# One more tile pair by seven block products in the first group of each MLP

## The chip, the cores and the metric

One core of a Trainium2 chip runs the whole program, once. Its engines each work through a list of their own, in order: TensorE (PE) multiplies, VectorE (DVE), ScalarE (ACT) and GpSimd (POOL) work element by element, SyncE (SP) issues the loads. The metric is the device time of one execution in microseconds (us), as a median over runs.

## The reference, cut to what matters

Three blocks follow one another on 528 tokens (16 meta tokens and 512 real ones) of width 1024: differential attention, latent attention, and a mixer with convolution and window attention. Behind each stands the same gated MLP, and the change is in these three MLPs alone:

```python
xn = rms_norm(h, g_norm)
a, b = jnp.split(xn @ w_in, 2, axis=-1)          # w_in: 1024 x (2 * 2816)
a_conv = conv_b + sum(ap[:, j:j + L] * conv_w[j] for j in range(3))   # along the tokens
return h + (jax.nn.silu(a_conv) * b) @ w_out     # w_out: 2816 x 1024
```

The 2816 hidden features are 22 tiles of 128. A tile pair is tile f of `a` together with tile f of `b`: two products of a 1024 x 128 weight tile with all tokens.

## The kernel before, in words

Features lie on the 128 partitions and tokens along the row. The normalised rows are divided by their root mean square only after the product, by a row R. Every operand of a large product is held as a high part and the remainder (`whi`/`wlo`, `Xh`/`Xl`), and a product is three matmuls: high by high, high by low, low by high. ACT casts the high part of a weight (line 176), DVE or POOL subtracts for the low part (lines 184 and 114).

An MLP is `ffn` (line 519). Its 22 tile pairs run in four groups, listed in the table `GROUPS` (line 61); behind each group its part of the second product (`group_h`) is added to h. A number in the table is a **plain** pair (class `Plain`): 2 tiles x 2 token halves x 8 chunks of 128 inputs x 3 matmuls = 96 matmuls of 256 to 264 columns. Pair 0 is a plain pair of its own form, `opening`, which also works out R. A tuple goes through `turns` (line 705): its last member is a plain pair, the others are of class `Seven`. A Seven pair takes the two weight tiles, the two halves of the 1024 inputs and the two token halves as a 2 x 2 by 2 x 2 product of blocks and makes it with seven block products in place of eight. A block product (`block`, line 565) is 4 chunks x 3 = 12 matmuls, so a Seven pair has 84. Its steps are named p1 to p7 in the code; p1 and p5 come first.

The seven products need sums and differences on both sides:

- Of the weights: `plan_ffn` loads four tiles' worth as kinds "a", "s", "t", "d"; `combine` (line 132) lets POOL add and subtract raw halves (`rawS`, `raw_0`, `raw_1`), and `_split` casts them. A Seven pair has 3.5 tiles to split where a plain pair has 2.
- Of the tokens: `differences` (line 540) makes, once for each MLP, four combinations of the blocks of X for k = 0 to 3: ACT scales (line 545), DVE makes `d` (lines 552, 553, 556, 557), ACT casts it into `Th` (562), DVE writes the remainder into `Tl` (563). p5 is the first step that reads `Th` and `Tl`: the first combination for all four k, in order of k. p1 reads X itself.

What sets the order: PE's instructions of `opening` and of each `turns` stand as they are written. The order of ACT, DVE, POOL and SP, and of PE elsewhere, is laid down when the program is built, by a scheduler that works from its own estimates; on the chip each engine then goes strictly through its list and waits on semaphores. Weights pass through 3 raw buffers and 4 split buffers; "s" and "d" have one buffer of their own.

The work of the other lines named below: 608 and 632 multiply the product in PSUM by R (`am`), 581, 585, 588 and 589 are the convolution, SiLU and R of the gate (`ct`), 612 and 642 multiply by the other tile's product, 450 and 451 split the result (`Gh`, `Gl`).

```python
u = [Seven(f, f - k0) for f in fs[:-1]]
v = Plain(fs[-1], fs[-1] - k0)
x, y = u[0], u[-1]
x.p1(), x.p5(), v.a(0), x.p6(), x.p2(), v.a(1), x.p7()
if x is y:
    v.b(0), x.p3(), x.p4(), v.b(1)
    return
x.p3(), y.p1(), x.p4(), y.p5(), y.p6(), y.p2(), v.b(0), y.p7(), y.p3(), v.b(1), y.p4()
```

Of the kernel before, what the change touches and what calls it, by code (L numbers as in the profile page):

```python
# [42 lines left out]
def _layout_params():  # L43
# [15 lines left out]
NPAR = _layout_params()  # L59

GROUPS = (
    (0, 5, (0, 1, 2, (3, 4))),
    (5, 10, ((5, 6, 7), (8, 9))),
    (10, 16, ((10, 11, 12), (13, 14, 15))),
    (16, 22, ((16, 17, 18), (19, 20, 21))),
# [1897 lines left out]
```

## Time and profile before

| | |
|---|---|
| median of 3 runs | 2063.59 us (2060.54 to 2064.36) |
| the profiled execution | 2064.14 us, of which 2062.4 us are the span from the first to the last instruction |
| PE busy | 2036.0 us, 99% of the span |
| DVE, ACT, POOL busy | 68%, 48%, 35% of the span |
| granted TensorE clock | 0.995 of 2.4 GHz on average |

The page gives busy time by engine. The chain of waits, in order of time, says which engine the end was waiting for at each moment. The timeline lists single instructions with start and length; the windows give busy time in a stretch. An engine that is busy 68% of the span on average may still be full in one stretch.

### The profile page before, as it was taken

What the parts mean: (1) busy time and instruction counts of PE and PEld (TensorE: products, weight loads), DVE (VectorE), ACT (ScalarE), POOL (GpSimd) and SP (SyncE); (2) the same over time, 40 slices, a digit from 0 to 9 for tenths busy, and PEclk for the clock granted to TensorE, in tenths of its full rate; (3) what the DMA queues carried; (4) which work ended last, traced back from release to release, by engine and by line L of the source; (5) the groups of instructions that cost most, each with busy time, mean ns of one, the idle gap of its engine ahead of it and who ended that gap; (6) DMA issues with size and microseconds to landing.
All of it is one profiled execution on the core that took longest, in us unless ns stands there. A gap on an engine that the chain in (4) does not pass through costs nothing.

```text
span 2062.4 us, 36284 instructions
## 1 busy us (share of the span) xinstructions
PE 2036.0 (99%) x14314; PEld 1884.8 (91%) x14314; DVE 1400.2 (68%) x2548; ACT 980.5 (48%) x1967; POOL 719.1 (35%) x818
## 2 busy tenths in 40 slices
PE   8999999999999999999999999999999999999998
PEld 8999899999999989899899898888888889999897
DVE  8788768667677576668667687675433358667684
ACT  6666545434355455455435355454332335445353
POOL 5222252435353331132536355321022242436452
PEclk9999999999999999999999999999999999999999
DMA  5121132333323111032332322222223232322322
GB/s 172 53 62 52 42 105 68 106 93 98 99 84 98 53 41 42 32 99 74 100 102 92 110 85 89 87 92 72 67 81 104 97 113 70 105 93 99 116 72 72
DMA packets 56426, 174.91 MB, mean 85 GB/s; under 512 B 6464, under 2 KB 9408, under 8 KB 56256
## 3 DMA queue, kind: packets, MB, share of 16 engines
q1 hardware_dynamic: 55824, 172.34, 26.4%
q8 instruction: 112, 1.84, 0.4%
q14 instruction: 58, 0.48, 0.1%
q10 hardware_dynamic: 432, 0.27, 0.0%
HBM read 170.45 MB, written 2.10 MB: 84 GB/s over the span
## 4 chain that ended last, share of the span: by engine, by line
PE 87%; DVE 8%; ACT 2%; issue 1%; POOL 1%; DMA 0%; ACTq 0%; DVEq 0%; SPq 0%
PE po L343 24%; PE pf L576 18%; PE pf L343 17%; PE pc L343 6%; PE pg L343 4%; PE pyc L343 2%; PE pq L343 2%; PE s L767 2%; DVE wlo L184 2%; PE ph L343 2%; PE pm L343 2%; PE pd L343 1%; PE o L1422 1%; PE pya L343 1%; DVE nm L777 1%
## 5 line engine op out<-in xcount | busy, mean ns | idle before, releaser
L176 ACT CAST whi<-raw 128x512 fp32r<-128x512 f32 (+4 forms) x484 | 384.7, 808 | 532.9 <-PE po L343 154.5
L114 POOL TENSOR_TENSOR wlo<-raw,whi 128x256 fp32r<-128x256 f32 (+1 forms) x316 | 273.9, 894 | 572.7 <-ACT whi L176 537.3
L184 DVE TENSOR_TENSOR wlo<-raw,whi 128x512 fp32r<-128x512 f32 (+2 forms) x590 | 410.7, 731 | 50.6 <-ACT whi L176 47.3
L343 PE MATMUL pf<-Xl,whi 128*128 128x256 f32 (+2 forms) x960 | 271.2, 283 | 0.9 <-DVE Xl L454 0.9
L343 PE MATMUL pf<-Xh,whi 128*128 128x256 f32 (+2 forms) x960 | 271.4, 283 | 0.0
L343 PE MATMUL pf<-Xh,wlo 128*128 128x256 f32 (+2 forms) x960 | 271.4, 283 | 0.0
L343 PE MATMUL po<-Gh,wlo 128*128 128x512 f32 (+2 forms) x710 | 239.4, 338 | 0.0
L343 PE MATMUL po<-Gl,whi 128*128 128x512 f32 (+2 forms) x710 | 238.5, 337 | 0.0
L343 PE MATMUL po<-Gh,whi 128*128 128x512 f32 (+2 forms) x710 | 235.6, 340 | 0.0
L343 PEld LDWEIGHTS pf<-Xl,whi 128*128 128x128 f32 x960 | 181.3, 189 | 1.2 <-DVE Xl L454 1.1
L343 PEld LDWEIGHTS pf<-Xh,whi 128*128 128x128 f32 x960 | 181.6, 189 | 0.0
L343 PEld LDWEIGHTS pf<-Xh,wlo 128*128 128x128 f32 x960 | 181.6, 189 | 0.0
L576 PE MATMUL pf<-Tl,whi 128*128 128x264 f32 (+2 forms) x576 | 162.4, 282 | 0.0
L576 PE MATMUL pf<-Th,whi 128*128 128x264 f32 (+2 forms) x576 | 162.3, 282 | 0.0
L576 PE MATMUL pf<-Th,wlo 128*128 128x264 f32 (+2 forms) x576 | 162.3, 282 | 0.0
L343 PEld LDWEIGHTS po<-Gh,wlo 128*128 128x128 f32 x710 | 133.5, 188 | 16.8
L343 PEld LDWEIGHTS po<-Gl,whi 128*128 128x128 f32 x710 | 133.6, 188 | 15.2
L343 PEld LDWEIGHTS po<-Gh,whi 128*128 128x128 f32 x710 | 132.5, 188 | 14.8
L576 PE MATMUL pf<-Xh,whi 128*128 128x264 f32 (+2 forms) x432 | 121.9, 282 | 0.0
L576 PE MATMUL pf<-Xh,wlo 128*128 128x264 f32 (+2 forms) x432 | 121.9, 282 | 0.0
L576 PE MATMUL pf<-Xl,whi 128*128 128x264 f32 (+2 forms) x432 | 121.9, 282 | 0.0
L585 DVE SCALAR_TENSOR_TENSOR ct<-am,par,ct 128x512 f32<-128x512 f32 (+4 forms) x132 | 114.5, 867 | 5.6 <-ACT ct L581 4.6
(434 smaller groups left out, 5496.3 us busy)
## 6 DMA issues: line engine op xcount, KB each, us to landing
raw<-in_w_in_dram SPq DMA_DIRECT2D x134, 512.0 KB, 3.5
raw<-in_w_up_dram SPq DMA_DIRECT2D x44, 512.0 KB, 3.3
raw<-in_w_qkv_dram SPq DMA_DIRECT2D x24, 512.0 KB, 3.6
raw<-in_w_out_dram SPq DMA_DIRECT2D x32, 384.0 KB, 3.2
raw<-in_w_out_dram SPq DMA_DIRECT2D x32, 320.0 KB, 2.9
raw<-in_w_o_dram SPq DMA_DIRECT2D x16, 512.0 KB, 3.5
raw<-in_w_dn_dram SPq DMA_DIRECT2D x16, 384.0 KB, 3.2
raw<-in_w_dn_dram SPq DMA_DIRECT2D x16, 320.0 KB, 2.9
```

The lines of the kernel that those rows point to most:

```text
L114: self.net.nc.gpsimd.tensor_tensor(d[:, c], a[:, c], b[:, c], op=op)
L176: nc.scalar.copy(h[:, c0 : c0 + z], r)
L184: nc.vector.tensor_tensor(l[:, c], r[:, a:b], h[:, c].bitcast(F32), op=ALU.subtract)
L343: nc.tensor.matmul(ps, w, x, start=first and i == 0, stop=i == len(ops) - 1, skip_group_check=not first)
L576: nc.tensor.matmul(ps[:, :H], a, b, start=first and i == 0, stop=i == len(ops) - 1, skip_group_check=not first)
L585: nc.vector.scalar_tensor_tensor(t[:, z:], am[:, a : a + n - z], w, t[:, z:], op0=ALU.mult, op1=ALU.add)
L767: nc.tensor.matmul(s[:, :w], qa[:, q0 : q0 + P], ka[:, k0:k1], start=z == 0, stop=z == len(ops) - 1 and not masked,)
L777: nc.vector.reduce_max(nm[:, j : j + 1], s[:, :w], axis=AX.X, negate=True)
L1422: nc.tensor.matmul(o[:, i, j, :], st[n, "pt", j][:, b * P : (b + 1) * P], V[:, b, c], start=n % 4 == j == b == 0, stop=False,)
```

## The change: the first group's table

```diff
 GROUPS = (
-    (0, 5, (0, 1, 2, (3, 4))),
+    (0, 5, (0, 1, (2, 3, 4))),
     (5, 10, ((5, 6, 7), (8, 9))),
     (10, 16, ((10, 11, 12), (13, 14, 15))),
     (16, 22, ((16, 17, 18), (19, 20, 21))),
```

Pair 2 of each MLP turns from a plain pair into a Seven pair. It takes its turns with Seven pair 3 and plain pair 4, in the form that (5, 6, 7) has already. Two plain pairs, 0 and 1, are left ahead of the first Seven pair, in place of three.

PE in the first MLP, where plain pair 1 ends (`pf` are the products; whi_4084 is pair 1's second weight). Before:

```order
L343 MATMUL pf_4314<-Xh_3587,wlo_4085 128x264
L343 MATMUL pf_4357<-Xh_3587,whi_4214 128x264
...
L343 MATMUL pf_4449<-Xh_3587,wlo_4280 128x264
L576 MATMUL pf_4485<-Xh_3587,whi_4343 128x264
...
L576 MATMUL pf_4508<-Th_4006,whi_4415 128x264
L576 MATMUL pf_4508<-Tl_4007,whi_4415 128x264
```

PE at the same place now (whi_4216 is pair 2's "a" weight, whi_4288 its "s" weight):

```order
L343 MATMUL pf_4322<-Xh_3587,wlo_4085 128x264
L576 MATMUL pf_4358<-Xh_3587,whi_4216 128x264
...
L576 MATMUL pf_4383<-Th_4006,whi_4288 128x264
L576 MATMUL pf_4383<-Tl_4007,whi_4288 128x264
```

The 96 matmuls of plain pair 2 are gone from between pair 1 and the first p1; p5, the first reader of `Th` and `Tl`, now stands 12 matmuls behind pair 1.

DVE in the first MLP, at the end of the differences (d_4203 and d_4204 are those of k = 3; Tl from d_4203 is the last that p5 needs). Before:

```order
L563 TENSOR_TENSOR Tl_4007<-d_4180,Th_4006 128x2x264
L563 TENSOR_TENSOR Tl_4007<-d_4191,Th_4006 128x2x264
L563 TENSOR_TENSOR Tl_4007<-d_4192,Th_4006 128x2x264
L556 TENSOR_TENSOR d_4203<-d_4204,x_4201 128x264
L184 TENSOR_TENSOR wlo_4501<-raw_1_4286,whi_4500 128x512
L184 TENSOR_TENSOR wlo_4501<-raw_0_4284,whi_4500 128x512
L585 SCALAR_TENSOR_TENSOR ct_4273<-am_4213,par,ct_4273 128x527
L557 SCALAR_TENSOR_TENSOR d_4204<-h,par,d_4203 128x264
L632 TENSOR_TENSOR am_4342<-pf_4357,R_4008 128x264
L632 TENSOR_TENSOR am_4342<-pf_4383,R_4008 128x264
L563 TENSOR_TENSOR Tl_4007<-d_4203,Th_4006 128x2x264
```

DVE now (d_4205 and d_4206 are those of k = 3, d_4193 and d_4194 of k = 2):

```order
L184 TENSOR_TENSOR wlo_4399<-raw_0_4379,whi_4398 128x512 x2
L553 SCALAR_TENSOR_TENSOR d_4206<-h,par,x_4203 128x264
L556 TENSOR_TENSOR d_4193<-d_4194,x_4191 128x264
L556 TENSOR_TENSOR d_4205<-d_4206,x_4203 128x264
L557 SCALAR_TENSOR_TENSOR d_4194<-h,par,d_4193 128x264
L632 TENSOR_TENSOR am_4215<-pf_4230,R_4008 128x264
L632 TENSOR_TENSOR am_4215<-pf_4256,R_4008 128x264
L557 SCALAR_TENSOR_TENSOR d_4206<-h,par,d_4205 128x264
L563 TENSOR_TENSOR Tl_4007<-d_4193,Th_4006 128x2x264
L563 TENSOR_TENSOR Tl_4007<-d_4205,Th_4006 128x2x264
```

From the first `am` (line 608) to the last `Tl` that p5 needs, DVE had 43 instructions and now has 37: gone from this stretch are two of line 184, two of line 632, one of line 585 and one of line 563. In the second MLP it is 44 and 39 (three of line 184 and two of line 632 fewer), in the third 43 and 39 (three of line 184 and two of line 632 fewer, one of line 585 more).

POOL in the first MLP, from the weights of the first Seven pair on (raw_0_4284 and raw_1_4286 are pair 3). Before:

```order
L114 TENSOR_TENSOR rawS_4348<-raw_1_4286 128x256 x2
L114 TENSOR_TENSOR wlo_4616<-raw_1_4286,whi_4615 128x256 x2
L400 TENSOR_TENSOR nr_4057<-nv_4055,mhalf 128x5
L114 TENSOR_TENSOR rawS_4995<-raw_1_4954 128x256 x2
L114 TENSOR_TENSOR raw_1_4286<-raw_0_4284,raw_1_4286 128x256 x2
L114 TENSOR_TENSOR raw_0_4284<-rawS_4348,raw_0_4284 128x256 x2
L114 TENSOR_TENSOR raw_0_4284<-raw_0_4284 128x256 x2
```

POOL now (4091 and 4093 are pair 2, 4379 and 4381 pair 3):

```order
L114 TENSOR_TENSOR rawS_4221<-raw_1_4093 128x256 x2
L114 TENSOR_TENSOR wlo_4500<-raw_1_4093,whi_4499 128x256 x2
L400 TENSOR_TENSOR nr_4057<-nv_4055,mhalf 128x5
L114 TENSOR_TENSOR rawS_4403<-raw_1_4381 128x256 x2
L114 TENSOR_TENSOR raw_1_4093<-raw_0_4091,raw_1_4093 128x256 x2
L114 TENSOR_TENSOR raw_1_4381<-raw_0_4379,raw_1_4381 128x256 x2
L114 TENSOR_TENSOR raw_0_4091<-rawS_4221,raw_0_4091 128x256 x2
L114 TENSOR_TENSOR raw_0_4091<-raw_0_4091 128x256 x2
L114 TENSOR_TENSOR rawS_5013<-raw_1_4972 128x256 x2
L114 TENSOR_TENSOR raw_0_4379<-rawS_4403,raw_0_4379 128x256 x2
L114 TENSOR_TENSOR raw_0_4379<-raw_0_4379 128x256 x2
```

The pairs' sums stand in one more set: pair 2's four additions of `raw_0` come ahead of pair 3's. Over the program PE's list is 36 rows shorter, 12 for each MLP; DVE's is 15 longer, ACT's 24, POOL's 16 (rows as counted with equal neighbours merged); SP issues as many loads of the same sizes as before.

## Rows read from the trace of the kernel before

**Rows 1.** The page, busy us (share of the span) and instructions by engine:

```profile
PE 2036.0 (99%) x14314; PEld 1884.8 (91%) x14314; DVE 1400.2 (68%) x2548; ACT 980.5 (48%) x1967; POOL 719.1 (35%) x818
```

**Rows 2.** Windows (us, busy PE, PEld, DVE, ACT, POOL; clock; DMA): pairs 1-2; group two:

```profile
311.65:335.06 23.41, 23.41 (x195) 23.41 (x195) 23.30 (x45) 15.82 (x25) 3.55 (x4) 1.00 0.18 54
935.86:958.84 22.98, 22.98 (x195) 22.98 (x195) 22.84 (x44) 15.09 (x24) 3.52 (x4) 1.00 0.21 60
1706.94:1729.55 22.61, 22.61 (x194) 22.61 (x194) 21.81 (x41) 14.87 (x23) 6.73 (x8) 1.00 0.15 44
...
386.18:440.12 53.94, 53.94 (x447) 53.94 (x446) 39.25 (x62) 25.86 (x45) 23.86 (x26) 1.00 0.31 93
```

**Rows 3.** Chain of waits in order of time (start us, us, what):

```profile
311.65 23.40 PE pf L343 x192
335.06 2.89 PE pf L576 x24
...
926.18 8.66 PE pf L343 x72
935.86 22.98 PE pf L343 x192
958.84 2.87 PE pf L576 x24
...
1695.93 10.12 PE pf L343 x72
1706.94 22.61 PE pf L343 x192
...
1790.32 9.89 PE pf L576 x84
```

**Rows 4.** Timeline of DVE, first MLP (start us, us of all, line, what):

```profile
312.83 0.77 DVE L608 TENSOR_TENSOR am<-pf,R 128x264 f32<-128x264 f32 x2
...
315.81 0.76 DVE L585 SCALAR_TENSOR_TENSOR ct<-am,par,ct 128x526 f32<-128x526 f32 x1
316.49 0.70 DVE L563 TENSOR_TENSOR Tl<-d,Th 128x528 fp32r<-128x528 f32 x1
317.11 0.43 DVE L552 TENSOR_TENSOR d<-x 128x264 f32<-128x264 f32 x1
...
320.35 1.29 DVE L184 TENSOR_TENSOR wlo<-raw,whi 128x512 fp32r<-128x512 f32 x2
321.55 0.77 DVE L612 TENSOR_TENSOR ct<-pf,ct 128x264 f32<-128x264 f32 x2
322.24 0.99 DVE L557 SCALAR_TENSOR_TENSOR d<-h,par,d 128x264 f32<-128x264 f32 x1
323.15 0.97 DVE L556 TENSOR_TENSOR d<-d,x 128x264 f32<-128x264 f32 x1
324.04 1.24 DVE L563 TENSOR_TENSOR Tl<-d,Th 128x528 fp32r<-128x528 f32 x1
...
333.95 0.76 DVE L632 TENSOR_TENSOR am<-pf,R 128x264 f32<-128x264 f32 x2
334.63 0.69 DVE L563 TENSOR_TENSOR Tl<-d,Th 128x528 fp32r<-128x528 f32 x1
```

**Rows 5.** Timeline of POOL, first MLP:

```profile
321.17 1.77 POOL L114 TENSOR_TENSOR raw<-rawS,raw 128x256 f32<-128x256 f32 x2 [11.52 <-issue]
322.90 1.82 POOL L114 TENSOR_TENSOR raw<-raw 128x256 f32<-128x256 f32 x2
```

**Rows 6.** Timeline of DVE, second and third MLP, the same `Tl`:

```profile
959.26 0.67 DVE L563 TENSOR_TENSOR Tl<-d,Th 128x516 fp32r<-128x516 f32 x1
...
1730.12 0.68 DVE L563 TENSOR_TENSOR Tl<-d,Th 128x512 fp32r<-128x512 f32 x1
```

**Rows 7.** Windows around a gap of PE in attention:

```profile
44.80:48.20 3.40, 1.60 (x13) 1.26 (x11) 3.38 (x9) 1.53 (x6) 1.75 (x1) 1.00 0.53 148
48.20:51.60 3.40, 3.05 (x13) 2.73 (x14) 2.22 (x5) 3.16 (x10) 0.20 (x1) 0.50 0.02 6
```

## The prediction

> **What bounds the kernel now.** I read the page first: PE is busy 2036.0 us of a span of 2062.4 [rows 1], so whatever PE does not have to do is saved, and whatever makes PE wait is added. DVE's 68% there is an average, and an average says nothing about one place. So the second view was the windows of the stretch that the change shortens, plain pairs 1 and 2 of each MLP. There PE is busy without a break, and so is DVE: 23.30 of 23.41 us in the first MLP, 22.84 of 22.98 in the second, 21.81 of 22.61 in the third [rows 2]. Two engines are full side by side, and the change takes half of PE's work out of this stretch. The third view, the chain of waits in order of time, shows that today PE alone ends it: 23.40 us of plain matmuls and at once p1 and p5 [rows 3]. The fourth was the timeline of DVE, for the moment at which what p5 reads is ready.
>
> **What is removed.** Seven block products have 84 matmuls where a plain pair has 96. One matmul costs its spacing in a solid run: 2.89 us / 24 = 0.120 us in the first MLP, 2.87 / 24 = 0.120 in the second, 9.89 / 84 = 0.118 in the third [rows 3]. So 12 fewer save 1.44 + 1.44 + 1.41 = 4.29 us in all. That is 0.21% of the time, just at the 0.2% that a measurement of this kernel can tell from no change.
>
> **What is moved: the token differences come due one plain pair earlier.** p5 needs the first combination for k = 0 to 3. Its 11th matmul is the first that reads the last piece, `Tl` of k = 3, and p1's 12 stand ahead of it, so it is due 22 matmuls after p1 begins. Today:
>
> - First MLP: p1 begins at 335.06, so it is due at 335.06 + 22 x 0.1204 = 337.71. It is ready at 334.63 + 0.69 = 335.32 [rows 3, 4]. Margin 2.39 us.
> - Second: due at 958.84 + 22 x 0.1196 = 961.47, ready at 959.93 [rows 3, 6]. Margin 1.54 us.
> - Third: p1 begins at 1706.94 + 22.61 = 1729.55, so it is due at 1732.14, and ready at 1730.80 [rows 3, 6]. Margin 1.34 us.
>
> The change makes it due one plain pair sooner: 23.40 / 2 = 11.70, 22.98 / 2 = 11.49 and 22.61 / 2 = 11.31 us [rows 3]. Were DVE's list as before, p5 would wait 9.31, 9.95 and 9.97 us, together 29.2. That is the upper bound for the order.
>
> The list is not as before: five or six instructions that stood ahead of the last `Tl` now stand behind it or are gone. Their price is the distance to the next row's start: 1.20 for two of line 184 (320.35 to 321.55), 0.68 for the two of line 632 (333.95 to 334.63), 0.68 for one of line 585 (315.81 to 316.49), 0.62 for one of line 563 (316.49 to 317.11) [rows 4]. First MLP: 1.20 + 0.68 + 0.68 + 0.62 = 3.18. Second: 3 x 0.60 + 0.68 = 2.48. Third: 1.80 + 0.68 - 0.68 = 1.80. The waits come to 6.13, 7.47 and 8.17 us, together 21.8. No slack takes them up: PE runs in order, everything of the MLP is queued behind p5, and PE is busy in every one of these windows.
>
> **What is added beside it.** POOL's additions of raw weights slow DVE. While POOL ran four of them from 321.17 to 324.7 [rows 5], DVE's rows of lines 557, 556 and 563 took 0.99, 0.97 and 1.24 us, and from 322.24 to 325.20 they fill 2.96 us [rows 4]. Undisturbed, line 563 takes 0.62 from start to start; line 552, of the size of 556 and 557, takes 0.43, less the 0.08 by which rows overlap (0.70 against 0.62): 0.62 + 2 x 0.35 = 1.32. So one pack of four costs DVE 1.64 us. In the first MLP POOL's list now has two such packs where it had one, the first for pair 2 and the second for pair 3, and both are due while DVE makes the differences. I add one pack there: 7.77 in place of 6.13, and 23.41 us of waiting in all. For the bounds: no pack at all would take 3 x 1.64 = 4.9 off the 21.77 (16.9); one more pack in each MLP and no help from the order would make it 29.23 + 4.9 = 34.1.
>
> The two rows of line 612, which read PSUM, ran beside the same pack at 0.77 us for both, as fast as those of line 608 [rows 4, 5]. The Trainium skill (SBUF — State Buffer, Who interferes with whom) says that a DVE instruction with two inputs in SBUF and a GpSimd instruction that reads SBUF lock each other out, and that whichever comes second is fully blocked until the first ends. The rows agree on who is slowed; on how much they show less, 1.64 us for a pack of 1.77 + 1.82 = 3.59. By the full lock the extra pack would cost 3.59, an estimate, and the time would be 2 us above my forecast.
>
> **The clock.** While PE waits for p5 it is nearly idle. In attention there is a stretch of 3.40 us in which PE was busy 1.60; the granted clock was 1.00 in it and 0.50, the lower level, in the next 3.40 us [rows 7]. What one such spell costs full PE work shows in the third MLP's opening: 72 matmuls of 256 columns took 10.12 us there, where 72 x 0.1177 = 8.47 is the full rate (and 8.66 is what 72 took in the second MLP) [rows 3]. I take 1.65 us for one spell, once in each MLP: 4.95 us. Bounds: none, or two spells each (9.9).
>
> **What I cost at nothing.** ACT casts 1.5 tiles more and makes four copies out of PSUM more in each MLP, DVE has five rows more, POOL eight additions more. Behind p5 they lie beside PE: group two has two Seven pairs by turns already, and PE is busy 53.94 of 53.94 us there with DVE at 39.25, ACT at 25.86, POOL at 23.86 [rows 2]. If that cover fails it is the third rival. Loads keep their number and sizes, some are issued earlier, and the DMA engines are at a share of 0.15 to 0.21 in the stretch [rows 2].
>
> **The sum.** 23.41 - 4.29 + 4.95 = +24.1 us on the profiled execution's 2064.14, which is 0.55 above the median of the runs shown: 2063.59 + 24.1 = 2087.7 us.
>
> **The rivals.**
>
> - The waits, but no spell of the lower clock: the 6 to 9 matmuls that run as `Th` and `Tl` arrive piece by piece might keep it up. Against it: most of 7 to 8 us is idle, more than in the stretch of rows 7. 2063.59 + 19.1 = 2082.7.
> - No wait at p5: the differences are ready in time, and only the 4.29 us are left, 2059.3. This is the other side. It is decided at one place: in the first MLP the last `Tl` would have to be written by 337.71 - 11.70 = 326.0, so DVE would have to do its 37 rows from line 608 on in 326.0 - 312.8 = 13.2 us. For it: the differences read only h and the gains, not R, so nothing in the mathematics ties them there. Against it: DVE's list still has all of line 552 behind line 608, which waits for R, and the 37 rows without any POOL beside them are 335.32 - 312.83 - 3.18 - 1.64 = 17.7 us.
> - The wait passes on: pair 3's "a" and "s" weights are late as well, because ACT's and DVE's lists have fallen behind. Price in each MLP: one pack of POOL, 3.59, and one pair of line 184, 1.20 [rows 4, 5], so 14.4 more: 2102.0. Against it: group two, where the same order of steps runs without a gap.
> - No change: waits of about 1.4 us in each MLP cancel the saving. It needs three quarters of the computed waits to vanish, and nothing in the rows does that.
>
> That the change doesn't do what it says is excluded by PE's list, 36 matmuls shorter.
>
> **How the numbers follow.** Forecast 0.66, waits without the clock 0.17, passed on 0.11, no wait 0.03, no change 0.03. The lowest sum of the bounds is 16.9 - 4.29 = +12.6 (2076.2), the highest 34.1 - 4.29 + 9.9 = +39.7 (2103.3). The range from 2076 to 2098 leaves out the no-wait and no-change cases and most of the passed-on case, some 0.15 together. Slower 0.94, same 0.03, faster 0.03.
>
> **What would show it.** In the profile after: three waits of PE, each right behind 12 matmuls of line 576 in the first group, at p5's matmuls, ended by line 563 of DVE or 562 of ACT, of 5 to 10 us in sum in each MLP; a granted clock of 0.50 just behind each; DVE without idle time from line 608 to there; PE with 36 matmuls fewer and no other new wait. If PE runs through p5 without a gap, the step that compares due and ready is wrong. If the waits are there and the time is above 2098, the cover of pair 3's weights failed.

## The result, and the profile after

| | before | after |
|---|---|---|
| median, runs in one session | 2062.55 us (2060.54 to 2064.36, 4 runs) | 2098.05 us (2097.52 to 2098.82, 4 runs) |
| ratio | | 1.0175 (95%: 1.0162 to 1.0188) |
| span of the profiled execution | 2062.4 us | 2097.0 us |
| granted TensorE clock, mean | 0.995 | 0.987 |

The change costs 35.5 us; 24.1 were forecast, and 2098.05 lies just beyond the end of the range, 2098. The first section of the page answers to [rows 1]: 36 matmuls fewer, and yet 5 us more of busy PE, because matmuls ran at the lower clock, as shown below.

```profile
PE 2041.0 (97%) x14278; PEld 1886.5 (90%) x14278; DVE 1416.9 (68%) x2559; ACT 988.7 (47%) x1991; POOL 748.4 (36%) x844
```

In the page's table of the costliest groups (busy us, mean ns, idle before and its releaser) two lines of `block` now carry waits; before both had 0.0:

```profile
L576 PE MATMUL pf<-Tl,whi 128*128 128x264 f32 (+2 forms) x624 | 177.8, 285 | 16.3 <-DVE Tl L563 16.2
L576 PE MATMUL pf<-Th,whi 128*128 128x264 f32 (+2 forms) x624 | 177.2, 284 | 12.4 <-ACT Th L562 12.3
```

That is 28.5 us (16.2 and 12.3) of PE standing idle for `Tl` and `Th`: 8.3, 10.6 and 9.6 in the three MLPs by the single gaps. The rest shows in the chain of waits in order of time, which answers to [rows 3] (start us, us, what): the end of p5, and the first 24 plain matmuls behind it.

```profile
333.72 1.47 PE pf L576 x5
335.19 4.79 PE pf L343 x24
...
972.81 0.80 PE pf L576 x2
973.61 4.68 PE pf L343 x24
...
1753.58 0.80 PE pf L576 x2
1754.38 5.03 PE pf L343 x24
```

And from the timeline of PE, for each MLP, the first matmul of p1 and the first of plain pair 4 (line 343):

```profile
322.13 0.28 PE L576 MATMUL pf<-Xh,whi 128*128 128x264 f32 x1
334.99 0.42 PE L343 MATMUL pf<-Xh,whi 128*128 128x264 f32 x1
...
957.50 0.28 PE L576 MATMUL pf<-Xh,whi 128*128 128x258 f32 x1
973.41 0.42 PE L343 MATMUL pf<-Xh,whi 128*128 128x258 f32 x1
...
1739.66 0.28 PE L576 MATMUL pf<-Xh,whi 128*128 128x256 f32 x1
1754.18 0.41 PE L343 MATMUL pf<-Xh,whi 128*128 128x256 f32 x1
```

p1 and p5 are 24 matmuls, 2.89, 2.87 and 2.83 us at the full rate. They took 334.99 - 322.13 = 12.86, 973.41 - 957.50 = 15.91 and 1754.18 - 1739.66 = 14.52. So plain pair 4's first piece came 10.0, 13.0 and 11.7 us late, 34.7 in all. (Both starts are taken from the timeline: the chain counts a piece from the end of the one before it and so gives starts some 0.2 us later.) Its 24 matmuls then took 4.79, 4.68 and 5.03 us (chain) for the same 2.89, 2.87 and 2.83: another 5.9. The windows from p5's release on show why (us, busy PE, PEld, DVE, ACT, POOL, clock, DMA):

```profile
335.20:340.00 4.80, 4.80 (x26) 4.80 (x26) 3.16 (x6) 1.65 (x3) 0.00 (x0) 0.58 0.00 0
973.60:978.30 4.70, 4.70 (x27) 4.70 (x26) 1.72 (x4) 0.99 (x2) 0.00 (x0) 0.58 0.00 0
1754.40:1759.40 5.00, 5.00 (x26) 5.00 (x26) 1.70 (x4) 0.99 (x2) 0.00 (x0) 0.52 0.00 0
```

PE is busy throughout at a granted clock of 0.5 to 0.6, mostly its lower level of 1.2 GHz, right behind the waits. The account: -4.3 for 36 matmuls, +34.7, +5.9, together +36.3, against 34.6 between the two spans. The trace of before has two spells of the lower clock that the trace of after lacks: in the third MLP's opening [rows 3] (74 matmuls in 10.00 us, in 8.50 after) and in 27 matmuls early in the mixer (7.90 us, 6.31 after), 3.1 us together. They are not put down to the change. Among the kernels below whose p5 doesn't wait, the third opening's 72 matmuls take 10.12 us in e10 and 8.59 in e11. Taken off, they bring the account to 33.2; no single new wait above 1 us makes the 1.4 us that are left.

**Why p5 is so late.** The windows from the first `am` (line 608) to the last `Tl` of p5:

```profile
312.38:334.27 21.89, 13.48 (x103) 12.76 (x102) 21.04 (x39) 13.71 (x22) 6.93 (x8) 0.88 0.22 64
951.61:972.76 21.15, 10.50 (x73) 9.10 (x72) 21.12 (x41) 13.10 (x21) 8.01 (x6) 0.79 0.20 65
1732.26:1753.53 21.27, 11.71 (x87) 10.52 (x85) 21.13 (x41) 13.10 (x21) 6.57 (x6) 0.81 0.20 65
```

DVE is all but full in all three, as forecast. But POOL works 6.6 to 8.0 us beside it, where it worked about 3.5 us in the first two MLPs of before; in the third it was 6.7 already [rows 2]. The timelines of POOL and DVE in the first MLP answer to [rows 5] and [rows 4]:

```profile
325.13 1.84 POOL L114 TENSOR_TENSOR rawS<-raw 128x256 f32<-128x256 f32 x2 [11.39 <-DMA raw<-in_w_in_dram]
327.95 1.98 POOL L114 TENSOR_TENSOR raw<-rawS,raw 128x256 f32<-128x256 f32 x2 [0.97 <-DVE wlo L184]
329.89 1.79 POOL L114 TENSOR_TENSOR raw<-raw 128x256 f32<-128x256 f32 x2
```

```profile
325.44 0.95 DVE L553 SCALAR_TENSOR_TENSOR d<-h,par,x 128x264 f32<-128x264 f32 x1
326.32 0.95 DVE L552 TENSOR_TENSOR d<-x 128x264 f32<-128x264 f32 x1
327.19 1.28 DVE L184 TENSOR_TENSOR wlo<-raw,whi 128x512 fp32r<-128x512 f32 x2
328.39 0.95 DVE L553 SCALAR_TENSOR_TENSOR d<-h,par,x 128x264 f32<-128x264 f32 x1
329.26 1.82 DVE L556 TENSOR_TENSOR d<-d,x 128x264 f32<-128x264 f32 x2
331.01 0.96 DVE L557 SCALAR_TENSOR_TENSOR d<-h,par,d 128x264 f32<-128x264 f32 x1
```

Six rows of the differences beside POOL take 0.87 us each from start to start, where such rows take 0.34 to 0.41 without it. The two of line 184 start in POOL's pause at 327 and take their usual 1.20.

The second cause lies ahead of line 608. ACT in the second MLP, before and after:

```profile
934.77 1.04 ACT L176 CAST whi<-raw 128x1024 fp32r<-128x1024 f32 x1 [4.66 <-PE pf L343]
935.77 0.66 ACT L420 COPY R<-st 128x512 f32<-128x512 f32 x2
```

```profile
948.01 1.57 ACT L176 CAST whi<-raw 128x512 fp32r<-128x512 f32 x2 [6.72 <-POOL raw L114]
949.49 0.65 ACT L420 COPY R<-st 128x512 f32<-128x512 f32 x2
```

In ACT's list a cast of pair 2's "s" weight, which reads POOL's difference, now stands ahead of the copy of R. It waits for POOL until 948.01, and the copy of R, without which line 608 can't begin, starts 3.5 us behind the start of pair 1 (957.50 less one plain pair of 11.49 is 946.01); before it started as pair 1 began (935.86 [rows 3]). Line 608 of DVE in the second and third MLP of before, and in all three after:

```profile
937.05 0.75 DVE L608 TENSOR_TENSOR am<-pf,R 128x256 f32<-128x256 f32 x2
...
1707.60 0.76 DVE L608 TENSOR_TENSOR am<-pf,R 128x256 f32<-128x256 f32 x2 [4.97 <-ACT R L420]
```

```profile
310.52 1.93 DVE L184 TENSOR_TENSOR wlo<-raw,whi 128x512 fp32r<-128x512 f32 x2 [4.53 <-ACT whi L176]
312.38 0.76 DVE L608 TENSOR_TENSOR am<-pf,R 128x264 f32<-128x264 f32 x2
...
948.66 3.02 DVE L184 TENSOR_TENSOR wlo<-raw,whi 128x512 fp32r<-128x512 f32 x3 [5.29 <-ACT whi L176]
951.61 0.74 DVE L608 TENSOR_TENSOR am<-pf,R 128x256 f32<-128x256 f32 x2
...
1729.87 2.47 DVE L184 TENSOR_TENSOR wlo<-raw,whi 128x512 fp32r<-128x512 f32 x3 [5.05 <-ACT whi L176]
1732.26 0.74 DVE L608 TENSOR_TENSOR am<-pf,R 128x256 f32<-128x256 f32 x2
```

R is not the last thing that line 608 waits for. In the second MLP its copy ends at 949.49 + 0.65 = 950.14, but DVE's own list has three rows of line 184 ahead of line 608. The first of them starts when that same cast is done, and they last until 951.61. In the third it is the same, with R ready at 1731.3 and line 608 at 1732.26. So the one cast that waits for POOL holds up ACT's list and DVE's. In the first MLP no such cast stands ahead of R; there two rows of line 184 take 1.86 us beside POOL's sums of pair 2 (POOL works from 310.04 to 313.75), where they took 1.21 before (311.62 to 312.83).

### The profile page after: what moved, and what is told of

It is laid out like the page before. It is cut to its first block, busy times and chain, and to the rows that moved or that the text cites. A ratio compares the mean times of both kernels' runs of the same rounds, so it can differ in the third digit from the quotient of the medians.

```text
span 2097.0 us, 36283 instructions
## 1 busy us (share of the span) xinstructions
PE 2041.0 (97%) x14278; PEld 1886.5 (90%) x14278; DVE 1416.9 (68%) x2559; ACT 988.7 (47%) x1991; POOL 748.4 (36%) x844
## 4 chain that ended last, share of the span: by engine, by line
PE 83%; DVE 11%; ACT 3%; issue 1%; POOL 1%; DMA 1%; ACTq 0%; POOLq 0%; DVEq 0%; SPq 0%
PE po L343 23%; PE pf L576 18%; PE pf L343 12%; PE pc L343 6%; PE pg L343 4%; DVE wlo L184 2%; PE pq L343 2%; PE pyc L343 2%; PE s L767 2%; PE pm L343 2%; PE ph L343 2%; PE pd L343 1%; PE o L1422 1%; PE pya L343 1%; DVE nm L777 1%
## 5 line engine op out<-in xcount | busy, mean ns | idle before, releaser
L343 PE MATMUL pf<-Xl,whi 128*128 128x256 f32 (+2 forms) x864 | 246.3, 285 | 0.9 <-DVE Xl L454 0.9
L343 PE MATMUL pf<-Xh,whi 128*128 128x256 f32 (+2 forms) x864 | 246.7, 286 | 0.0
L343 PE MATMUL pf<-Xh,wlo 128*128 128x256 f32 (+2 forms) x864 | 246.2, 285 | 0.0
L576 PE MATMUL pf<-Tl,whi 128*128 128x264 f32 (+2 forms) x624 | 177.8, 285 | 16.3 <-DVE Tl L563 16.2
L576 PE MATMUL pf<-Th,whi 128*128 128x264 f32 (+2 forms) x624 | 177.2, 284 | 12.4 <-ACT Th L562 12.3
L576 PE MATMUL pf<-Th,wlo 128*128 128x264 f32 (+2 forms) x624 | 176.7, 283 | 0.0
L343 PEld LDWEIGHTS pf<-Xl,whi 128*128 128x128 f32 x864 | 165.6, 192 | 1.2 <-DVE Xl L454 1.1
L343 PEld LDWEIGHTS pf<-Xh,whi 128*128 128x128 f32 x864 | 165.8, 192 | 0.1
L343 PEld LDWEIGHTS pf<-Xh,wlo 128*128 128x128 f32 x864 | 165.7, 192 | 0.0
L576 PEld LDWEIGHTS pf<-Tl,whi 128*128 128x128 f32 x624 | 118.2, 189 | 18.2 <-DVE Tl L563 18.2
```

The costliest lines, as they stand in the source:

```text
L343: nc.tensor.matmul(ps, w, x, start=first and i == 0, stop=i == len(ops) - 1, skip_group_check=not first)
L576: nc.tensor.matmul(ps[:, :H], a, b, start=first and i == 0, stop=i == len(ops) - 1, skip_group_check=not first)
```

## The experiments

Times are medians with their range and number of runs, and the ratio to the kernel before of the same session (2060.8 to 2062.6 us). Where two kernels of different sessions are compared, the ratios say it better than the times, and both are given. "Late" is how much later p5 ends than 24 matmuls behind p1's start, by the timeline. Line numbers of an edited kernel can stand some lines further down than in the kernel after.

**e1: plain pair 4 first.** Pair 4's four pieces go ahead of p5 in the first group, so that `Tl` is due about where it was.

```diff
+ if k0 == 0:
+     x.p1(), v.a(0), v.a(1), v.b(0), v.b(1), x.p5(), x.p6(), x.p2(), x.p7()
+     x.p3(), y.p1(), x.p4(), y.p5(), y.p6(), y.p2(), y.p7(), y.p3(), y.p4()
+     return
```

> Thirteen Seven pairs as in the changed kernel, but in the first group all four pieces of the plain pair stand between p1 and p5, so that the differences come due 96 matmuls (11.3 to 11.7 us) later again. Theory A (p5 is due before DVE has made the differences, and that alone costs): the waits at p5, 28.5 us in the changed kernel, and the low clock behind them go, and the 36 saved matmuls stay: 2058 to 2063 us. Theory B (the weights of the extra Seven pair, with their sums and splits, are what comes late): the same weights are made at the same time, so well over 2080 us, with PE waiting for weights.

Measured: 2073.69 (2072.38 to 2076.28, 5), ratio 1.0060 (1.0048 to 1.0073). Neither number. The waits for `Tl` and `Th` are gone (0.3 us are left in the third MLP), so the due time was right; other waits came in their place, 8.8 us in the first groups of the three MLPs. In the second MLP (waits of PE: total us, times, longest):

```profile
PE pf L578 <- ACT u L680: 3.2, 1, 3.2
PE pf L345 <- DVE am L634: 1.1, 1, 1.1
```

With two Seven pairs by turns and no plain piece between them, PE overtakes ACT's copies out of PSUM (line 680 here), which stand in ACT's list behind casts that wait for POOL.

**e2: the place alone.** Twelve Seven pairs, but p5 behind two plain pairs as in the changed kernel.

```diff
-    (0, 5, (0, 1, (2, 3, 4))),
+    (0, 5, (0, 1, (3, 4), 2)),
```

> Twelve Seven pairs as in the kernel before, but the first group's table reads (0, 1, (3, 4), 2): the Seven pair comes one plain pair earlier and plain pair 2 behind it. Theory A: nearly all of the loss without the saving: waits at p5 of 20 to 28 us in the three MLPs, the low clock 8 to 12 us, so 2091 to 2102 us. Theory B: as many weights are split as before, so 2060 to 2066 us.

Measured: 2091.38 (2089.95 to 2095.05, 4), ratio 1.0142 (1.0127 to 1.0158). The gaps at p5 are 6.2, 6.2 and 6.4 us. So moving p5 one plain pair forward makes most of the loss without any thirteenth pair. The rest, 28.5 against 18.8 us of gaps, goes along with pair 2's own weights, whose sums e4 takes out.

**e3: the clock alone.** 60, 92 and 84 dummy matmuls ahead of pair 2's p5, to fill the wait.

```diff
+ if me.f == 2:
+     for z in range({"w_in0": 60, "w_in1": 92, "w_up": 84}[wi]):
+         nc.tensor.matmul(me.C[:, :H], me.wa[0][:, z % 4, :], X.at(z % 4, *quads[0])[0], ...)
```

> The changed kernel with idle matmuls (60, 92 and 84 of them in the three MLPs, their result overwritten by p5) ahead of p5's, in the time in which PE waits. If the low clock behind the waits costs what is left of the loss after waits and saving (35.5 - 28.5 + 4.3, some 10 to 11 us), PE keeps the upper level and the time falls to 2086 to 2090 us. If the low clock lies beside the waiting and costs nothing, 2097 to 2100 us.

Measured: 2092.18 (2091.29 to 2093.69, 4), ratio 1.0149 (1.0135 to 1.0163). In the first MLP pair 4's piece now runs at the full rate (chain of waits):

```profile
335.36 2.89 PE pf L343 x24
```

In the second and third it does too, 2.89 and 2.83 us, so the clock behind p5 costs the 5.9 us read above. The time is also 5.9 us below the changed kernel (5.4 by the ratios, 7.4 between the profiled spans), but that it is the same number is luck. In the trace three things add up: 5.9 gained behind p5; p5 itself 9.7, 11.5 and 9.9 us late, 3.6 less in all, mostly because DVE begins line 608 1.4 and 2.3 us earlier in the second and third MLP; and 1.5 lost again, because the third opening's 72 matmuls take 10.12 us here. Together that is 8.0, beside the 7.4 between the spans. So this is not the clock alone. The 10 to 11 expected here were wrong: they took p5's own crawling matmuls for clock cost too, but these wait for `Tl` anyway.

**e4: no sums.** POOL's `combine` leaves out its additions for pairs 2 and 3.

```diff
-            if kind == "a":
+            if kind == "a" and key[1] in (2, 3):
+                self.rows[-1].append(self.rows[-1][1][:, slice(0, 512)])
+            elif kind == "a":
```

> The changed kernel without POOL's sums of the raw weights of pairs 2 and 3 in each MLP: these pairs' weights are then not the sums that the seven products need, everything else runs. If POOL slows DVE's differences by about half a microsecond for each row beside it (0.87 in place of 0.34 to 0.40 in the profile of the changed kernel), the waits shrink by 2 to 4 us in each MLP and the clock recovers sooner: 2084 to 2092 us. If it is only 1.6 us for a pack, as forecast: 2090 to 2095 us. If DVE's own list is all that counts: 2097 to 2099 us.

Measured: 2087.09 (2084.95 to 2090.83, 4), ratio 1.0126 (1.0112 to 1.0140). p5 is 11.5 us less late in sum, the gaps fall from 28.5 to 18.0, and the time by 10.1 (ratios) to 11.0 us. DVE begins line 608 (610 here) 1.3, 1.3 and 1.6 us behind pair 1's start, near the 1.3, 1.3 and 0.9 of before, in place of 2.0, 5.6 and 4.0: R and the rows of line 184 are no longer held up. That is 7.4 of the 11.5; the other 4.2 are the stretch from line 608 on. The forecast had its POOL packs in that stretch alone, one in each MLP as before and one extra in the first, 4 x 1.64 = 6.6.

**e5, e6, e7, e8: the differences earlier.** e5 writes `differences()` ahead of `opening`; e6 does so with the table of before; e7 leaves the third MLP as it was; e8 puts only the one of k = 0 early in the third MLP.

```diff
+            differences()
             with self.in_order():
                 opening()
-            differences()
```

> The change's table, with the token differences (line 540) written ahead of `opening`, so that DVE and ACT are free to make them before the row R is known. Theory (DVE comes to the differences too late, POOL's sums slow what is left): with nothing of them due behind R the p5 waits go in all three MLPs, 28 us, and the half clock with them: 2057 to 2060. In the third MLP the differences now share DVE with the last splits of X (line 454), and PE may wait there instead; that is at most some 3 us, so up to 2063. Rival (what is late is the weights' split, or ACT, and the differences only stand beside it): waits of 5 us or more in each MLP stay at p5, 2080 or more.

> Control for the run before: the same edit with the table of before (twelve pairs by seven). Both theories: its p5 never waited, so nothing is to be gained; 2062 (same as before), or up to 3 us more where the differences stand in the way of the third MLP's opening. The distance to the run before is what the 36 fewer matmuls are worth when p5 does not wait: 4.3 us if all is hidden.

> The change's table, the differences ahead of `opening` in the first and second MLP alone; the third as in the changed kernel. Theory: the first two MLPs lose their waits and spells (10.4 and 13.5 us of the change's cost), the third keeps its 10.7, less 1.4 for its matmuls everywhere: 2069 to 2073. Rival: 2085 or more.

> As e5, but in the third MLP only the difference of k = 0 stands ahead of `opening`, the other three behind it. Theory: the third MLP's opening is then disturbed less than in e5 (1 us or none) and its p5 still waits, for less than the 9.6 us of the changed kernel, some 3 to 6 us: 2061 to 2066. If it comes out under e5, the order of X's last splits against the differences decides in the third MLP; if above, p5's due time does.

Measured: e5 2077.88 (2076.60 to 2080.34, 4), ratio 1.0085 (1.0071 to 1.0099); e6 2078.14 (2075.72 to 2079.79, 5), 1.0084 (1.0070 to 1.0098); e7 2084.67 (2084.11 to 2085.30, 4), 1.0117 (1.0103 to 1.0131); e8 2080.28 (2078.09 to 2086.78, 5), 1.0103 (1.0086 to 1.0119). The waits for `Tl` and `Th` go wherever all differences stand first, as the theory says, and stay (8.0 and 5.5 us) in the third MLP of e7 and e8. The totals miss: the wait moved to the opening. The waits of PE in e5, second MLP, and in e6, first MLP:

```profile
PE pf L343 <- ACT R L420: 3.4, 1, 3.4
```

```profile
PE st L373 <- DVE acc L367: 3.0, 1, 3.0
```

DVE's last addition of squares for R, and then R, come late behind the differences. e6 pays this with twelve pairs as well. e5 is only 0.3 us faster than e6, where 4.3 were expected: its waits are 2.6 us longer, so even without a wait at p5 the 36 matmuls bring nothing here. At this place, ahead of the sums of squares, the differences push out something that PE needs. Whether another place would do isn't shown: in the changed kernel DVE stands idle for 4.5, 5.3 and 5.1 us just ahead of the rows of line 184 in front of line 608 (shown above), waiting for ACT, and the differences read only h, the gains and what ACT scales of them. No run put them there.

**e9: more POOL.** More additions into a tile that nobody reads, behind pair 2's sums.

```diff
+        if self.plan[self.ns][0][1] == 2:
+            x = self.more.tile([P, 512], F32, tag="rawX", ...)
+            for _ in range(4):
+                self.sums(x, a[0][:, lo], a[0][:, hi], ALU.add)
```

> The changed kernel with four more POOL additions (into a tile that nobody reads) behind those of pair 2 in each MLP, just as DVE starts on the row R and the differences. Theory (a DVE row with two operands in SBUF stands still while POOL adds): four additions are 3.6 us of POOL, and DVE, which has no idle time there, gives back up to that in each MLP, less what its rows from PSUM are spared: 2 to 3.6 us, 6 to 11 in all, 2104 to 2109 beside 2098. Rival (the forecast's price of 1.64 for a pack): 5 us, 2103. No effect of POOL on DVE: 2098.

Measured: 2108.02 (2105.14 to 2109.91, 4), ratio 1.0228 (1.0208 to 1.0248). Each of the four calls is two instructions, so POOL got eight, not four (timeline of POOL, first MLP):

```profile
313.78 8.21 POOL L114 TENSOR_TENSOR rawX<-raw 128x256 f32<-128x256 f32 x8
```

The first of DVE's rows beside it, and the first behind it:

```profile
314.29 0.96 DVE L556 TENSOR_TENSOR d<-x 128x264 f32<-128x264 f32 x1
...
322.20 0.48 DVE L557 SCALAR_TENSOR_TENSOR d<-h,par,x 128x264 f32<-128x264 f32 x1
```

The eight rows from 314.29 to 322.20, none of which reads PSUM, take 7.9 us; the same eight take 3.8 in the changed kernel (314.22 to 318.03). So DVE lost 4.1 us to 8.2 of POOL, 0.50 for one. The forecast's 1.64 for 3.59 is 0.46: its price was right. The total agrees, with a wide margin: 10.0 us (10.9 by the ratios, give or take 5) for 23.9 us of POOL in the three MLPs. p5 is 3.2 us later in the first MLP, where 0.85 of DVE's loss fills a wait for ACT that it had there, and 6.9 later in all three. By the expectation's 3.6 us of POOL the total seemed to confirm a full standstill; by what really ran, it doesn't. The Trainium skill (SBUF — State Buffer, Who interferes with whom) has the later of the two instructions fully blocked; single rows here are held by 0.5 us, and POOL's additions are held too, 1.03 us each where four take 2.84, 0.71 each, without DVE beside them (the changed kernel at 307.23), so that DVE loses half of POOL's longer time.

**e10, e11: the thirteenth pair elsewhere.** First group as before; in group two pairs 8 and 9 are both Seven, by turns without a plain one (e10), or all five in one sequence with plain 7's last piece inside pair 8 (e11).

```diff
-    (5, 10, ((5, 6, 7), (8, 9))),
+    (5, 10, ((5, 6, 7), (8, 9, None))),    # e10
+    (5, 10, ((5, 6, 8, 9, 7),)),           # e11
```

> The first group as before the change; the thirteenth pair in the second group instead: pairs 8 and 9 both by seven products, by turns without a plain one. Theory (the thirteenth pair costs time only because the differences are not made yet and DVE is full in the first group): the 36 fewer matmuls are saved, 4.3 us, 2057 to 2059, or less by what the weights of 8 and 9 come late, as p7's weight did at 3 us where two pairs by seven stood without a plain one between: up to 2067. Rival (a thirteenth pair without plain pieces beside it cannot be fed anywhere): 2068 or more.

> The thirteenth pair in the second group as in the run before, but pairs 5, 6, 8, 9 (by seven) and plain 7 in one sequence: plain 7's last piece stands between p5 and p6 of pair 8, and p1 of pair 9 between p2 and p7 of pair 8, so that ACT's copies out of PSUM have 24 matmuls of cover more. Theory: the run before lost its 4.3 us to two waits of 1.3 to 1.7 us for ACT's copies in each MLP; with the cover these go and 36 matmuls are saved: 2057 to 2059 beside 2061.5. Rival (DVE's, ACT's or POOL's list is behind for good in that group): waits move to the next pair and the time stays at 2065 to 2070.

Measured: e10 2070.04 (2069.72 to 2070.95, 5), ratio 1.0043 (1.0030 to 1.0056); e11 2069.16 (2065.57 to 2070.29, 7), 1.0034 (1.0020 to 1.0047). No wait for `Th` or `Tl`, no lower clock behind p5: the loss of 35 us is a matter of the first group. But the matmuls saved, 1.4 us in each MLP, are eaten by waits for ACT's copies. Waits of PE in group two of the first MLP, e10 and then e11:

```profile
PE pf L579 <- ACT u L669: 1.7, 1, 1.7
PE pf L579 <- ACT u L681: 1.4, 1, 1.4
```

```profile
PE pf L579 <- ACT u L681: 1.3, 1, 1.3
```

e11 took one of the two waits away, as expected, not both. Its profiled execution is only 1.4 us longer than that of before (span 2063.8), its median 7.5. That execution is the fastest of the seven, and it lacks the two spells of the lower clock that the trace of before has (3.1 us, above); for the rest no trace shows a reason.

**e12 to e16: R ahead of the cast.** In e12 the second half of pair 2's "s" cast is scaled by a column of ones that is computed from R, so ACT has to copy R first.

```diff
+ self.W.one = self.nrm.tile([P, 1], F32, tag="one", ...)
+ nc.scalar.activation(self.W.one, R[:, t0 : t0 + 1], AF.Identity, scale=0.0, bias=self.ones[:, :1])
...
+ if kind == "s" and key[1] == 2 and c0:
+     nc.scalar.activation(h[:, c0 : c0 + z], r, AF.Identity, scale=self.one)
```

e13 makes that tile 64 bytes wide. e14 puts only the column into the kernel before. e15 and e16 are e12 and e14 with the column in an existing tile, `self.ones[:, 5:6]`.

> The changed kernel, with one cast of pair 2's weights (ACT's second half of "s", which reads POOL's difference) made to depend on the row R, so that ACT's list has R's copy (line 420) ahead of it in the second and third MLP, as it already is in the first. Theory (in the changed kernel DVE begins the stretch from line 608 to p5's last Tl later, counted from the start of pair 1: 2.0, 5.6 and 4.0 us against 1.3, 1.3 and 0.9 before, because R stands behind that cast, which waits for POOL): the second and third MLP get back up to 4.3 and 3.1 us, the first nothing: 2090 to 2093 beside 2098. Rival (POOL slows DVE as much whenever R comes, so an earlier start is used up by slower rows): 2096 to 2098, with line 608 early and the stretch longer.

> As the run before (one cast of pair 2 behind R), with its helper column in a tile of 64 bytes for each partition in place of 4. There the MLP fronts of the second and third MLP had gained 1.8 and 1.5 us of p5's lateness, but PE took 1 to 2% longer for the same 512-column matmuls of the mixer at a granted clock of 1.00, some 5 us, and 1 us more elsewhere. Theory (the 4 bytes moved the tiles behind them to addresses that PE reads more slowly): without the shift only the gain is left, 2094 to 2096 beside 2098. Rival (the slower stretches have another cause): again 2102 to 2104.

> Control: the kernel before the change with that helper column of 4 bytes, written once for each MLP and read by nobody. Theory of the addresses: 5 to 6 us slower than before, spread over the matmuls of the mixer and the later stages, without a wait. Rival: the same time as before, within 1 us.

> As e12 (one cast of pair 2 made to wait for R), with the helper column written into a column of an existing tile of ones, so that no tile is added and nothing moves in the memory. Theory: without slower matmuls only the earlier R is left; the sum of p5's lateness falls by about 2.8 us (34.3 to 31.5 in e12), 2094 to 2096 beside 2098. Rival (the added instruction on ACT disturbs, not the tile): 2101 or more.

> Control: the kernel before the change with that same column write, no tile added, read by nobody. If the added tile made e14 slower by 8 us: the time of before within 1 us. If the instruction itself did: 2068 to 2071 again.

Measured: e12 2103.35 (2102.57 to 2103.73, 5), ratio 1.0202 (1.0188 to 1.0216); e13 2102.55 (2100.55 to 2103.00, 5), 1.0196 (1.0182 to 1.0210); e14 2070.14 (2067.79 to 2071.88, 5), 1.0040 (1.0028 to 1.0053); e15 2094.85 (2094.44 to 2097.77, 4), 1.0165 (1.0152 to 1.0178); e16 2064.72 (2059.73 to 2066.60, 12), 1.0014 (1.0005 to 1.0022). e12 is slower than the changed kernel although p5 is less late. e14 shows that the added tile with its write costs the kernel before 8 us, and e16 that the write alone costs 3 to 4. Without the tile e15 came out where it was expected, 3.2 us below the changed kernel. By the ratios it is 2.1, and their intervals overlap, so what the earlier R is worth is read from the trace and not from the time. The timelines of ACT and DVE in its second MLP:

```profile
949.98 0.66 ACT L423 COPY R<-st 128x512 f32<-128x512 f32 x2
950.60 0.29 ACT L611 ACTIVATE ones<-R,ones 128x1 f32<-128x1 f32 x1
...
951.65 0.72 ACT L177 ACTIVATE whi<-raw,ones 128x512 fp32r<-128x512 f32 x1
```

```profile
952.10 0.74 DVE L613 TENSOR_TENSOR am<-pf,R 128x256 f32<-128x256 f32 x2
952.76 0.99 DVE L555 TENSOR_TENSOR d<-x 128x258 f32<-128x258 f32 x1
```

R comes first, and line 608 (613 here) starts 3.4 us earlier after pair 1's start in the second MLP, 1.9 in the third. Yet the way from there to p5's end is 1.5 and 0.3 us longer, since the first rows of the differences now run beside POOL's sums of pair 2 and take 0.9 us. p5 is 1.9 and 1.6 us less late, 0.5 more in the first MLP: of 5.3 us earlier start 3.0 are left. Both theories hold in part.

No kernel here beats the one before.

## Why the prediction was wrong

- *Removed: 4.29.* Right: 36 matmuls fewer at the same spacing.
- *Moved: the differences come due one plain pair earlier, and PE waits in each MLP behind 12 matmuls of line 576, for lines 562 and 563.* Right in place (at p5's matmuls, a few of which run ahead of the longest wait), cause and order of size. e1 shows the due time (with `Tl` due about where it was the wait is gone), e2 that the place alone makes two thirds of the gaps.
- *DVE's list from line 608 on is 6, 5 and 4 rows shorter, worth 7.46.* **This step failed, at its start.** It took line 608 to begin where it began before. In the trace of before p1 begins at 334.89, 958.68 and 1729.39 on the timeline; counted from line 608 to there, one plain pair taken off, DVE had 10.4, 10.1 and 10.5 us for the stretch. It now had 322.13 - 312.38 = 9.8, 957.50 - 951.61 = 5.9 and 1739.66 - 1732.26 = 7.4. So it began 0.6, 4.2 and 3.1 us late, 7.9 in all. In the second and third MLP a cast of pair 2 that waits for POOL stands ahead of R in ACT's list, and the row of line 184 for it ahead of line 608 in DVE's. e4 shows that POOL's sums are the cause: without them line 608 begins nearly where it did. e15 shows that R's place behind the cast is part of it: with R ahead, 5.3 us of the start come back, and 3.0 of them reach p5. The forecast read the rows from line 608 on, and not what stands ahead of it on ACT, DVE and POOL.
- *One extra pack of POOL, in the first MLP, 1.64.* **Put in the wrong place.** The price holds (e9: 0.50 us for one of POOL, the forecast 0.46). But pair 2's pack runs mostly ahead of line 608, in the first MLP until 313.75, and it does so in all three MLPs, where it delays the start above and not the rows of the differences. Within the stretch the error is small: 21.89, 21.15 and 21.27 us from line 608 to the last `Tl`, where 20.95, 20.40 and 21.40 follow from the forecast's numbers, 1.6 more in all.
- Together: p5 was forecast 23.4 us late and was 34.7. Of the 11.3, 7.9 are the later start, 1.6 the stretch, and 1.3 the last matmuls of p5, which ran at the lower clock (0.80 us for two in the chain in place of 0.24). The last 0.5 is in the forecast's due times: it took p1's starts from the chain, some 0.16 us behind the timeline in each MLP.
- *The clock: 4.95.* Right in place and nearly in size: 5.9 behind p5, where e3's filled waits bring the full rate back, and the 1.3 at p5's end beside it.
- *Costed at nothing: the work behind p5.* Held. The trace has no other new wait of PE above 1 us, so the rival in which pair 3's weights are late did not happen. The prediction's own test for it, waits at p5 and a time above 2098, names the wrong cause here: the time got there by a larger wait at p5.
- *The rival without a wait* failed as argued: from line 608 on DVE had next to no idle time. Ahead of line 608 it had some, 4.5 to 5.3 us in each MLP, but the list puts no differences there.

## What to carry to other kernels

When work is taken out of a stretch in which two engines are full, the other one sets the new length; the saving on the first is lost, and its waits can lower its clock on top. When an order is compared, read each engine's list from the last point that is surely unchanged, not from the first instruction of interest: here a single cast that waits for a third engine stood ahead of the first row counted in two lists, and in the second and third MLP the start came 7.3 us later, while the rows counted behind it were worth 4.3. And a helper added for an experiment needs a control of its own: here it hid the effect under a larger one.

## What the runs showed that was not expected

A tile of one column, added to a pool and read by nobody, made the same matmuls slower at a full clock. 24 matmuls of 512 columns in the mixer (chain of waits), in e14 with the added tile and in e16 with the same write into an existing one:

```profile
1329.27 5.60 PE pc L343 x24
```

```profile
1327.04 5.50 PE pc L343 x24
```

That is 1.8%, without a wait, at a granted clock of 1.00 in both; the later stages are longer too, and e14 is 5.4 us above e16. The tile's size makes no difference between 4 and 64 bytes (e13 is as slow as e12). That other tiles now lie at other addresses may be the cause; it was not tried by itself. e16 is still 0.14% above the kernel before, for which its trace (span 2062.6) shows no reason.
